# Last pair of down-projection rows: the two token halves of row 6 in separate PSUM tiles, its products in another order, all final multiplications on VectorE

## The chip, the core and the metric

The kernel runs on one core of a Trainium2 chip. The metric is the device time of one execution in microseconds. Three runs of the kernel before took 865.1, 865.74 and 865.78 us; the median is 865.74 us. The execution that the profiler recorded took 865.26 us, of which the span of its instructions covers 863.5 us; the 1.76 us around it belong to no instruction of the kernel.

## What is computed

One decoder block: a recurrent mixer, a state-space mixer, an output projection, a gated MLP, and a final RMSNorm. The change lies at the very end, in the MLP's down projection and the final norm:

```python
def conv_glu_ffn(h, w_up, conv_w, conv_b, w_down):
    u = causal_dwconv(h @ w_up, conv_w, conv_b)
    gate, val = jnp.split(u, 2, axis=-1)
    return (jax.nn.silu(gate) * val) @ w_down
...
    h = h + conv_glu_ffn(rmsnorm(h, norm2_w[l]), ...)
    y = rmsnorm(h, final_norm_w)
    return y[:, N_META:, :]
```

There are 512 tokens, 1024 model features and 2816 MLP features, all in float32.

## The kernel before

Features lie on the 128 partitions, tokens along the free axis. The 1024 model features make eight row tiles `hs[0]` to `hs[7]` (named `xr` in the profile), the 2816 MLP features make 22 tiles of the contraction. Every float32 product is made of three matmuls on rounded operands: weight-high times activation-high, weight-high times activation-low, weight-low times activation-high (`partial`, L1148 to L1150).

**Weights** come in chunks, in the order of the list `chunks`; `dn_chunks(p)` (L169 to L180) gives those of a pair of rows. A chunk passes three stages in `ahead` (L265): SyncE (SP) issues a DMA into a `raw` tile (L276), ScalarE (ACT) rounds it to `whi` (L199), VectorE (DVE) subtracts to get `wlo` (L200). Each of the three kinds of tile has three buffers. So the DMA of chunk n waits until `wlo` of chunk n-3 is made, and `whi` of chunk n waits until TensorE (PE) is through with chunk n-3. The next chunks are asked for two ahead of their use.

**Down projection.** Rows 0 and 1 are made plainly. Rows 2 to 7 are made in three pairs, p = 1, 2, 3 (loop at L1184, rows 2p and 2p+1). For the contraction tiles 8 to 19 a scheme with seven products is used in place of eight: chunks `d0` to `d6`, on halves of the 512 tokens, on sums of weights that were made in DRAM earlier (`sumsdn`), and on sums of activations (`dts`). The tiles 0 to 7 and 20, 21 go the plain way: chunks `qa` and `qb` for row 2p+1 at full width, chunks `ra` (8 tiles) and `rb` (2 tiles) for row 2p. The sums are:

- `x`: row 2p, first token half (first bank of a two-bank PSUM tile `pup`)
- `z`: row 2p, second token half (second bank of the same tile)
- `y`: a bank (`psn`) that is first set to a copy of `x` after `d0` (L1194), and whose content after `d2` is copied into `z` (L1200); with `s7` (copied from the bank `pv`) and `z` it gives the correction of row 2p+1 (L1207 to L1209)

For the last pair (`j == end`, rows 6 and 7) the list has `ra` and `rb` twice: `x` is finished first with one copy, then `z` gets `d4` and the other copy.

**Final norm.** When a row is complete, `squares` takes its square (L1174), multiplies it by the norm's weight (L1175) and adds the square to `facc` (L1177). Row 6 comes last and goes by token halves (L1228 to L1251): DVE adds the PSUM sum (L1231), ACT squares (L1232), PE sums over the partitions with a matrix of ones (L1235 for `facc`, L1236 for row 6), ACT takes logarithm and exponential (L1237, L1238), which gives `rs`, and eight rows are multiplied by `rs` into output tiles `ot`: rows 1 and 4 by GpSimd (POOL, L1247), row 6 by DVE with one more factor (L1244), the others by DVE (L1249). Two rows at a time go to DRAM by a 256 KB DMA, issued from SP for rows 0, 1 and 4, 5 and from ACT for rows 2, 3 and 6, 7 (L1251).

**What sets the order.** A scheduler places each engine's instructions before the program runs; on the chip each engine takes its own in that order. In the kernel before, the two adds of row 6 (L1231) stand side by side on DVE, behind all weight splits.

Of the kernel before, what the change touches and what calls it, by code (L numbers as in the profile page):

```python
# [11 lines left out]
ALU = mybir.AluOpType  # L12
# [12 lines left out]
KF = FF // P  # L25
# [18 lines left out]
C_FN = C_FB + 44  # L44
# [10 lines left out]
DN = 1, 2, 3  # L55
D0, DK = 8, 6
# [8 lines left out]
def tile_block(ctx: ExitStack, tc: tile.TileContext, xT, w_in, w_dt, w_out, w_up, w_down,  # L65
               par, consts, consti, out, dbg=None):
    nc = tc.nc
    V, A, G, PE = nc.vector, nc.scalar, nc.gpsimd, nc.tensor
# [9 lines left out]
    def slot(name, n=NT, dtype=F32, parts=P, tag="m"):  # L78
        return gp.tile([parts, n], dtype, tag=tag, name=name, bufs=TAGS[tag])
# [4 lines left out]
    def evac():  # L84
        return first(150000)

    def bank(name):
        return px.tile([P, 512], F32, tag="px", name=name)

    def banks2(name):  # L90
        return pj.tile([P, 1024], F32, tag="pj", name=name)
# [17 lines left out]
    def col(c):  # L109
        return pt[:, c:c + 1]  # L110
# [58 lines left out]
    def dn_chunks(p):  # L169

        j, j2, c1, c2, c3 = 2 * p, 2 * p + 1, D0 * P, (D0 + DK) * P, (D0 + 2 * DK) * P

        def summed(n):
            return lambda: sumd["dn", p][:, n * DK * P:(n + 1) * DK * P]

        rest = [(("ra", p), w_down[j][:, 0:c1], D0), (("rb", p), w_down[j][:, c3:], KF - D0 - 2 * DK)]
        r = [(("qa", p), w_down[j2][:, 0:c1], D0), (("d0", p), w_down[j][:, c1:c2], DK),
             (("qb", p), w_down[j2][:, c3:], KF - D0 - 2 * DK), (("d1", p), w_down[j][:, c2:c3], DK), (("d2", p), summed(0), DK),
             (("d3", p), summed(2), DK), (("d5", p), summed(1), DK), (("d6", p), w_down[j2][:, c2:c3], DK)]
        return r + (rest if p == DN[-1] else []) + [(("d4", p), summed(3), DK)] + rest  # L180

    for p in DN:
        chunks += dn_chunks(p)
# [81 lines left out]
    def ahead(n):  # L265
        while wnext[0] < min(n, len(chunks)):
            key, src, kc = chunks[wnext[0]]
            if key[0] in ("w0", "w1", "w2"):
                with first():
                    wdone[key] = scheme_weights(key)  # L270
                wnext[0] += 1
                continue
            with first(), ExitStack() as st:
                raw, hi, lo = raw_tiles(key)
                d = slice(0, kc * P)
                nc.sync.dma_start(raw[:, d], src() if callable(src) else src)  # L276
                if key[0] == "dn" and key[1] < 2 and not key[2]:
                    st.enter_context(tc.issue_after(last_s4[0].ins))
                split_weights(raw, hi, lo, d, V)
            wdone[key] = (hi, lo)  # L280
            wnext[0] += 1
# [13 lines left out]
    def weights(*key):  # L295
        if key in (("up", 0), ("up", KF)):
            return wdone.pop(key)
        used[0] += 1
        ahead(used[0] + 2)
        return wdone.pop(key)  # L300
# [29 lines left out]
    with first(200000):  # L330
        for k in range(0, KD, 2):
            d = slice(k * P, (k + 2) * P)
            for j, w, kx in ((BT, starts[0], k), (CT, starts[1], k + 1)):
                t = slot(f"x{kx}", tag="y")
# [37 lines left out]
    with first():  # L372
        for n, (a0, a1) in enumerate(((0, HALF), (HALF, NT))):
            p = bank(f"psn{n}")
# [4 lines left out]
        for k in range(KD):  # L379
            t = slot(f"xn{k}")  # L380
# [44 lines left out]
    for n, (a0, a1) in enumerate(((0, HALF), (HALF, NT))):  # L425
        p = bank(f"psd{n}")[0:66, :]
# [469 lines left out]
    hs, u2h, u2l = [], [], []  # L896
# [34 lines left out]
    u1 = []  # L931
# [69 lines left out]
    def product_banks(whole):  # L1001

        if not turn[0]:
            pairs.extend(banks2(f"pup{i}") for i in range(2))
        i = turn[0] % 2
        turn[0] += 1
        was, filled[i] = filled[i], whole
        return pairs[i], was
# [110 lines left out]
    dts = []  # L1119
    places = iter(["b1"] * 6 + ["L"] * 4 + ["u"] * 14)  # L1120
    first_half, second_half = slice(0, 256), slice(256, 512)
# [21 lines left out]
    def partial(ps, w, xs, start=False, stop=False):  # L1143

        for k, (xh, xl) in enumerate(xs):
            wh, wl = (t[:, k * P:(k + 1) * P] for t in w)
            one, end = start and k == 0, stop and k == len(xs) - 1
            PE.matmul(ps, wh, xh, start=one, stop=False, skip_group_check=True)  # L1148
            PE.matmul(ps, wh, xl, start=False, stop=False, skip_group_check=True)  # L1149
            PE.matmul(ps, wl, xh, start=False, stop=end, skip_group_check=True)  # L1150

    def gated(k0, kc, d):
        return [(ah[k][:, d], al[k][:, d]) for k in range(k0, k0 + kc)]

    def by_bank(t):
        return t.rearrange("p (a t) -> p a t", a=2)
# [25 lines left out]
    whole, K2, KR = slice(0, 512), D0 + DK, D0 + 2 * DK  # L1182
    end = 2 * DN[-1]
    for p in DN:  # L1184
        j, j2 = 2 * p, 2 * p + 1
        q = bank(f"pq{p}")
        partial(q[:], weights("qa", p), gated(0, D0, whole), start=True)
        xz, was = product_banks(True)
        assert was
        x, z, y, v = xz[:, first_half], xz[:, 512:768], u1[0][:, first_half], bank(f"pv{p}")[:, first_half]  # L1190
        sv, s7 = slot(f"dsv{p}", 512, tag="ab"), slot(f"ds7{p}", 256, tag="rs")
        partial(x, weights("d0", p), gated(D0, DK, first_half), start=True)
        with evac():
            A.activation(y, x, AF.Copy)  # L1194
        partial(q[:], weights("qb", p), gated(KR, KF - KR, whole), stop=True)
        V.tensor_tensor(hs[j2][:, META:], hs[j2][:, META:], q[:], ALU.add)
        partial(x, weights("d1", p), gated(K2, DK, first_half))
        partial(y, weights("d2", p), [t[1] for t in dts])
        with evac():
            A.activation(z, y, AF.Copy)  # L1200
        partial(v, weights("d3", p), [t[2] for t in dts], start=True, stop=True)
        with evac():
            A.activation(s7[:], v, AF.Copy)
        partial(z, weights("d5", p), [t[0] for t in dts])
        partial(y, weights("d6", p), [t[3] for t in dts], stop=True)
        with evac():
            V.tensor_tensor(sv[:, second_half], s7[:], z, ALU.add)  # L1207
            V.tensor_tensor(sv[:, first_half], s7[:], y, ALU.add)
        V.tensor_tensor(hs[j2][:, META:], hs[j2][:, META:], sv[:], ALU.subtract)  # L1209
        squares(j2)  # L1210

        def others(*sums):
            for key, k0, kc in (("ra", 0, D0), ("rb", KR, KF - KR)):
                w = weights(key, p)
                for ps, d in sums:
                    partial(ps, w, gated(k0, kc, d), stop=key == "rb")

        if j == end:
            others((x, first_half))
        partial(z, weights("d4", p), gated(K2, DK, second_half))  # L1220
        others(*([] if j == end else [(x, first_half)]), (z, second_half))
        if j < end:
            V.tensor_tensor(by_bank(hs[j][:, META:]), by_bank(hs[j][:, META:]), by_bank(xz[:])[:, :, first_half], ALU.add)
            squares(j)
            continue
        hh, halves, ps = hs[j], (0, 256), {0: x, 256: z}
        sq = slot(f"fsq{j}", 512, tag="pr")
        for d0 in halves:  # L1228
            d, dh = slice(d0, d0 + 256), slice(META + d0, META + d0 + 256)
            with evac():  # L1230
                V.tensor_tensor(hh[:, dh], hh[:, dh], ps[d0], ALU.add)  # L1231
                A.activation(sq[:, d], hh[:, dh], AF.Square)  # L1232
                p = bank(f"psn3_{d0}")
                rs = slot(f"rs{d0}", 256, tag="u")
                PE.matmul(p[:, 0:256], ones, acc[:, d], start=True, stop=False)  # L1235
                PE.matmul(p[:, 0:256], ones, sq[:, d], start=False, stop=True)  # L1236
                A.activation(rs[:], p[:, 0:256], AF.Ln, bias=eps[:], scale=1.0 / DM)  # L1237
                A.activation(rs[:], rs[:], AF.Exp, scale=-0.5)  # L1238
                pr = rs
                for k in range(0, KD, 2):  # L1240
                    ot = slot(f"ot{d0}_{k}", 512, tag="u")[:].rearrange("p (a t) -> p a t", a=2)
                    for i in range(2):
                        if k + i == end:
                            V.scalar_tensor_tensor(ot[:, i, :], hh[:, dh], col(C_FN + j), pr[:, 0:256],  # L1244
                                                   ALU.mult, ALU.mult)
                        elif k + i in (1, 4):
                            G.tensor_tensor(ot[:, i, :], hs[k + i][:, dh], rs[:], ALU.mult)  # L1247
                        else:
                            V.tensor_tensor(ot[:, i, :], hs[k + i][:, dh], pr[:, 0:256], ALU.mult)  # L1249
                    dst = out[k * P:(k + 2) * P, d].rearrange("(a p) t -> p a t", p=P)  # L1250
                    (nc.scalar if k % 4 else nc.sync).dma_start(dst, ot)  # L1251

# [64 lines left out]
```

## Time and profile before

| what | value |
|---|---|
| median of three runs | 865.74 us |
| the profiled execution's own time | 865.26 us |
| its span | 863.5 us |
| PE busy | 842.5 us (98% of the span) |
| DVE busy | 612.3 us (71%) |
| ACT busy | 485.7 us (56%) |
| POOL busy | 121.5 us (14%) |
| HBM read and written | 241 GB/s over the span |

A row of the timeline gives the start in microseconds from the span's start, the duration, the engine, the line, the operation, the tile written, the tiles read, and the sizes (partitions x elements). In brackets stands how long the engine had been idle, and what ended that. "SPq" and "ACTq" rows are the issue of a DMA, not its transfer. A row of the windows view gives a stretch, its length, the busy time of each engine with the number of instructions, the granted clock of PE as a share of full speed, and the busy share and rate of the DMA engines.

### The profile page before, as it was taken

What the parts mean: (1) busy time and instruction counts of PE and PEld (TensorE: products, weight loads), DVE (VectorE), ACT (ScalarE), POOL (GpSimd) and SP (SyncE); (2) the same over time, 40 slices, a digit from 0 to 9 for tenths busy, and PEclk for the clock granted to TensorE, in tenths of its full rate; (3) what the DMA queues carried; (4) which work ended last, traced back from release to release, by engine and by line L of the source; (5) the groups of instructions that cost most, each with busy time, mean ns of one, the idle gap of its engine ahead of it and who ended that gap; (6) DMA issues with size and microseconds to landing.
All of it is one profiled execution on the core that took longest, in us unless ns stands there. A gap on an engine that the chain in (4) does not pass through costs nothing. (4 is left out here: it accounts for less than half of the span.)

```text
span 863.5 us, 16958 instructions
## 1 busy us (share of the span) xinstructions
PE 842.5 (98%) x6908; PEld 812.9 (94%) x6908; DVE 612.3 (71%) x1036; ACT 485.7 (56%) x777; POOL 121.5 (14%) x160
## 2 busy tenths in 40 slices
PE   7999999999999999999999999999999999999994
PEld 6999899999999999999999999999999999889993
DVE  6984988799766666645353569878888888984554
ACT  8636985867444444454332345567666667653441
POOL 1321021222313131302222210000000000100001
PEclk9999999999999999999999999999999999999997
DMA  7598288783979598947987962365555555844552
GB/s 252 204 246 233 82 263 197 160 154 118 259 145 178 173 267 158 177 153 265 317 183 173 236 140 74 99 193 183 190 180 174 190 177 171 217 119 132 153 153 98
DMA packets 60143, 156.15 MB, mean 181 GB/s; under 512 B 6280, under 2 KB 10760, under 8 KB 60064
## 3 DMA queue, kind: packets, MB, share of 16 engines
q1 hardware_dynamic: 36704, 98.37, 34.7%
q0 software_dynamic: 20832, 53.09, 30.9%
q10 hardware_dynamic: 2528, 3.60, 1.3%
q8 instruction: 54, 0.88, 0.4%
q14 instruction: 25, 0.20, 0.1%
HBM read 152.89 MB, written 55.23 MB: 241 GB/s over the span
## 5 line engine op out<-in xcount | busy, mean ns | idle before, releaser
L322 PE MATMUL pj<-u_hi,whi_in 128*128 128x272 f32 (+1 forms) x752 | 156.6, 288 | 0.0
L322 PE MATMUL pj<-u_lo,whi_in 128*128 128x272 f32 (+1 forms) x752 | 156.5, 287 | 0.0
L322 PE MATMUL pj<-u_hi,wlo_in 128*128 128x272 f32 (+1 forms) x752 | 155.5, 286 | 0.0
L322 PEld LDWEIGHTS pj<-u_hi,whi_in 128*128 128x128 f32 x752 | 115.9, 188 | 2.8 <-issue 2.7
L322 PEld LDWEIGHTS pj<-u_lo,whi_in 128*128 128x128 f32 x752 | 116.0, 188 | 2.4 <-issue 1.8
L322 PEld LDWEIGHTS pj<-u_hi,wlo_in 128*128 128x128 f32 x752 | 116.3, 189 | 1.4 <-issue 1.3
L200 DVE TENSOR_TENSOR wlo_in<-raw_in,whi_in 128x1024 fp32r<-128x1024 f32 (+1 forms) x58 | 64.5, 1112 | 51.5 <-ACT whi_in L199 49.1
L199 ACT ACTIVATE whi_in<-raw_in 128x1024 fp32r<-128x1024 f32 (+1 forms) x58 | 56.1, 967 | 64.0 <-PE pj L322 59.1
L199 ACT ACTIVATE whi_w<-raw_w 128x1024 fp32r<-128x1024 f32 x54 | 57.2, 1058 | 26.4 <-PE pup L1052 13.3
L200 DVE TENSOR_TENSOR wlo_w<-raw_w,whi_w 128x1024 fp32r<-128x1024 f32 x54 | 66.0, 1222 | 6.4 <-ACT whi_w L199 5.8
L217 POOL COPY tick<-ticks 128x1 f32<-128x1 f32 x6 | 9.2, 1539 | 322.2 <-DVE ticks L216 322.2
L200 DVE TENSOR_TENSOR wlo_d<-raw_d,whi_d 128x768 fp32r<-128x768 f32 x21 | 20.1, 958 | 29.7 <-ACT whi_d L199 29.7
L1052 PE MATMUL psn<-t1l,whi_w 128*128 128x258 f32 x144 | 40.9, 284 | 0.0
L1053 PE MATMUL pup<-n_hi,wlo_w 128*128 128x258 f32 x144 | 40.8, 283 | 0.1
L1051 PE MATMUL pup<-n_hi,whi_w 128*128 128x258 f32 x144 | 40.8, 283 | 0.0
L1053 PE MATMUL psn<-t1h,wlo_w 128*128 128x258 f32 x144 | 40.7, 282 | 0.0
L1052 PE MATMUL pup<-n_lo,whi_w 128*128 128x258 f32 x144 | 40.6, 282 | 0.0
L1051 PE MATMUL psn<-t1h,whi_w 128*128 128x258 f32 x144 | 40.4, 280 | 0.0
L200 DVE TENSOR_TENSOR wlo_out<-raw_out,whi_out 128x1024 fp32r<-128x1024 f32 x16 | 19.6, 1225 | 26.4 <-ACT whi_out L199 26.4
L237 POOL DMA_DIRECT2D sums<-in_w_up_dram x18 | 21.2, 1179 | 114.6 <-issue 107.3
L199 ACT ACTIVATE whi_d<-raw_d 128x768 fp32r<-128x768 f32 x21 | 17.8, 848 | 32.9 <-PE pup L1149 15.6
L199 ACT ACTIVATE whi_out<-raw_out 128x1024 fp32r<-128x1024 f32 x16 | 16.9, 1055 | 25.9 <-PE pout L322 16.5
(459 smaller groups left out, 2570.5 us busy)
## 6 DMA issues: line engine op xcount, KB each, us to landing
sums<-in_w_up_dram POOLq DMA_DIRECT2D x54, 512.0 KB, 8.6
raw_in<-in_w_in_dram SPq DMA_DIRECT2D x50, 512.0 KB, 5.0
sums<-in_w_up_dram POOLq DMA_DIRECT2D x36, 256.0 KB, 7.9
raw_w<-in_w_up_dram SPq DMA_DIRECT2D x18, 512.0 KB, 3.5
raw_w<-sums SPq DMA_DIRECT2D x18, 512.0 KB, 4.0
raw_out<-in_w_out_dram SPq DMA_DIRECT2D x16, 512.0 KB, 6.5
sumsdn<-in_w_down_dram POOLq DMA_DIRECT2D x9, 768.0 KB, 8.1
sums<-sums POOLq DMA_DIRECT2D x18, 256.0 KB, 6.3
```

The lines of the kernel that those rows point to most:

```text
L199: A.activation(hi[:, d], raw[:, d], AF.Copy)
L200: eng.tensor_tensor(lo[:, d], raw[:, d], hi[:, d].bitcast(F32), ALU.subtract)
L217: gate = G.tensor_copy(tick[:], ticks[:, n:n + 1])
L237: G.dma_start(ds[j][:, 0:2], of[j][3], accum_op=ALU.add)
L322: PE.matmul(ps[:, O + a0:O + a1], w, x[:, a0:a1], start=s, stop=e)
L1051: PE.matmul(ps, wh, xh, start=first, stop=False, skip_group_check=True)
L1052: PE.matmul(ps, wh, xl, start=False, stop=False, skip_group_check=True)
L1053: last_product[:] = [PE.matmul(ps, wl, xh, start=False, stop=k == H - 1, skip_group_check=True)]
```

## The change

For the last pair alone: `z` moves into the other of the two `pup` tiles, so that `x` (`pup0`) and `z` (`pup1`) no longer share one. The weights that finish `x` get names and places of their own: `xb` (two tiles of the contraction) right behind `d1`, `xa` (eight tiles) behind `d5`. The products `d5` and `d6` swap places. So `x` is complete with `xa`, before `d4`. The count of matmuls, of weight chunks and of bytes stays the same. GpSimd's four multiplications go to DVE.

```diff
-        return r + (rest if p == DN[-1] else []) + [(("d4", p), summed(3), DK)] + rest
+        if p == DN[-1]:
+            r[6:8] = r[7], r[6]
+            xa, xb = [(key, *rest[n][1:]) for n, key in enumerate((("xa", p), ("xb", p)))]
+            r[4:4], r[9:9] = [xb], [xa]
+        return r + [(("d4", p), summed(3), DK)] + rest
...
-        x, z, y, v = xz[:, first_half], xz[:, 512:768], u1[0][:, first_half], bank(f"pv{p}")[:, first_half]
+        other = product_banks(True)[0] if j == end else xz
+        x, z, y, v = xz[:, first_half], other[:, 512:768], u1[0][:, first_half], bank(f"pv{p}")[:, first_half]
...
         partial(x, weights("d1", p), gated(K2, DK, first_half))
+        if j == end:
+            partial(x, weights("xb", p), gated(KR, KF - KR, first_half))
...
-        partial(z, weights("d5", p), [t[0] for t in dts])
-        partial(y, weights("d6", p), [t[3] for t in dts], stop=True)
+        for key in ("d6", "d5") if j == end else ("d5", "d6"):
+            if key == "d5":
+                partial(z, weights(key, p), [t[0] for t in dts])
+            else:
+                partial(y, weights(key, p), [t[3] for t in dts], stop=True)
...
         if j == end:
-            others((x, first_half))
+            partial(x, weights("xa", p), gated(0, D0, first_half), stop=True)
...
-                pr = rs
...
                         if k + i == end:
-                            V.scalar_tensor_tensor(ot[:, i, :], hh[:, dh], col(C_FN + j), pr[:, 0:256],
-                                                   ALU.mult, ALU.mult)
-                        elif k + i in (1, 4):
-                            G.tensor_tensor(ot[:, i, :], hs[k + i][:, dh], rs[:], ALU.mult)
+                            V.scalar_tensor_tensor(ot[:, i, :], hh[:, dh], col(C_FN + j), rs[:], ALU.mult, ALU.mult)
                         else:
-                            V.tensor_tensor(ot[:, i, :], hs[k + i][:, dh], pr[:, 0:256], ALU.mult)
+                            V.tensor_tensor(ot[:, i, :], hs[k + i][:, dh], rs[:], ALU.mult)
```

What this does to the order, at three places. First DVE, the end of its program before the change (`xr6` is row 6, `pup0` its PSUM tile, `ot0` and `ot256` the outputs of the first and the second token half, `rs0` and `rs256` their norms):

```order
L200 TENSOR_TENSOR wlo_ra_3_10145<-raw_ra_3_10143,whi_ra_3_10144 128x1024
L200 TENSOR_TENSOR wlo_rb_3_10157<-raw_rb_3_10155,whi_rb_3_10156 128x256
L1231 TENSOR_TENSOR xr6_5914<-xr6_5914,pup0_6048 128x256 x2
L1249 TENSOR_TENSOR ot0_0_10218<-xr0_5235,rs0_10213 128x256
L1249 TENSOR_TENSOR ot0_2_10222<-xr2_5418,rs0_10213 128x256
L1249 TENSOR_TENSOR ot0_2_10222<-xr3_5537,rs0_10213 128x256
L1249 TENSOR_TENSOR ot0_4_10226<-xr5_5785,rs0_10213 128x256
L1244 SCALAR_TENSOR_TENSOR ot0_6_10230<-xr6_5914,pt_75,rs0_10213 128x256
L1249 TENSOR_TENSOR ot0_6_10230<-xr7_6033,rs0_10213 128x256
L1249 TENSOR_TENSOR ot256_0_10242<-xr0_5235,rs256_10237 128x256
```

The same place with the change (its line numbers are a few higher: L1241 is the add that was L1231, L1255 and L1253 are the multiplications, L1181 is the sum into `facc`):

```order
L204 TENSOR_TENSOR wlo_ra_3_10127<-raw_ra_3_10125,whi_ra_3_10126 128x1024
L1181 TENSOR_TENSOR facc_9128<-facc_9128,fsq7_10121 128x512
L1241 TENSOR_TENSOR xr6_5914<-xr6_5914,pup0_6048 128x256
L204 TENSOR_TENSOR wlo_rb_3_10157<-raw_rb_3_10155,whi_rb_3_10156 128x256
L1255 TENSOR_TENSOR ot0_0_10218<-xr0_5235,rs0_10213 128x256
L1255 TENSOR_TENSOR ot0_0_10218<-xr1_5299,rs0_10213 128x256
L1255 TENSOR_TENSOR ot0_2_10222<-xr2_5418,rs0_10213 128x256
...
L1253 SCALAR_TENSOR_TENSOR ot0_6_10230<-xr6_5914,pt_75,rs0_10213 128x256
L1255 TENSOR_TENSOR ot0_6_10230<-xr7_6033,rs0_10213 128x256
L1241 TENSOR_TENSOR xr6_5914<-xr6_5914,pup1_6049 128x256
L1255 TENSOR_TENSOR ot256_0_10242<-xr0_5235,rs256_10237 128x256
```

The first half's add now stands ahead of the last weight split, all eight multiplications of the first half follow (those for rows 3 to 5 are left out here), and the second half's add stands behind them; `facc` is made behind the split of `ra`.

Second PE, with the change, from the end of `d4` on (`psn3_0` and `psn3_256` are the banks of the two sums over partitions, `cf` holds the ones):

```order
L1154 MATMUL pup1_6049<-ac19_hi_9032,wlo_d4_3_10096 128x256
L1152 MATMUL pup1_6049<-ac0_hi_7155,whi_ra_3_10126 128x256
L1153 MATMUL pup1_6049<-ac0_lo_7156,whi_ra_3_10126 128x256
L1154 MATMUL pup1_6049<-ac0_hi_7155,wlo_ra_3_10127 128x256
L1152 MATMUL pup1_6049<-ac1_hi_7287,whi_ra_3_10126 128x256
L1153 MATMUL pup1_6049<-ac1_lo_7288,whi_ra_3_10126 128x256
L1245 MATMUL psn3_0_10212<-facc_9128,cf_76 128x256
L1245 MATMUL psn3_256_10236<-facc_9128,cf_76 128x256
L1154 MATMUL pup1_6049<-ac1_hi_7287,wlo_ra_3_10127 128x256
L1152 MATMUL pup1_6049<-ac2_hi_7291,whi_ra_3_10126 128x256
```

Before the change the two sums over `facc` stood three matmuls ahead of the end of `d4`; now they stand five matmuls behind it. Three matmuls further on, behind `wlo_ra` of tile 2, comes the first half's sum over row 6 (L1246), which stood at the very end.

Third ACT, with the change, its last rows (L1242 is the square, L1247 and L1248 make `rs`):

```order
L203 ACTIVATE whi_ra_3_10126<-raw_ra_3_10125 128x1024
L1178 ACTIVATE fsq7_10121<-xr7_6033 128x512
L1179 ACTIVATE xr7_6033<-xr7_6033,pt_75 128x512
L203 ACTIVATE whi_rb_3_10156<-raw_rb_3_10155 128x256
L1242 ACTIVATE fsq6_10209<-xr6_5914 128x256
L1247 ACTIVATE rs0_10213<-psn3_0_10212,eps_78 128x256
L1248 ACTIVATE rs0_10213<-rs0_10213 128x256
L1257 DMA out_0_dram<-ot0_2_10222 128x2x256
L1257 DMA out_0_dram<-ot0_6_10230 128x2x256
L1242 ACTIVATE fsq6_10209<-xr6_5914 128x256
L1247 ACTIVATE rs256_10237<-psn3_256_10236,eps_78 128x256
L1248 ACTIVATE rs256_10237<-rs256_10237 128x256
```

The square of row 7 (L1178), which stood ahead of the split of the second `ra`, now stands behind it, and two output DMAs of the first half are issued ahead of the second half's square.

## The prediction

> **What bounds the kernel now.** I read the head of the page first: the span, and the share of PE.
>
> ```profile
> span 863.5 us, 16958 instructions
> PE 842.5 (98%) x6908; PEld 812.9 (94%) x6908; DVE 612.3 (71%) x1036; ACT 485.7 (56%) x777; POOL 121.5 (14%) x160
> ```
>
> PE is busy for 98% of the span, and the change adds or removes no matmul. So nothing is to be had while PE runs, unless PE is made to wait. What is left is the time behind the last matmul of the products. I therefore read the end of the chain of waits next (start, length, engine, tile, line).
>
> ```profile
> 845.04 0.86 PE psn L1235 x4
> 849.83 0.43 DVE xr L1231
> 850.28 0.42 ACT fsq L1232
> 850.75 0.71 PE psn L1236 x2
> 851.49 0.48 ACT rs L1237
> 852.00 0.43 ACT rs L1238
> 852.45 1.29 DVE ot L1249 x2
> 853.74 0.86 DVEq L1312
> 854.60 0.86 DVE ot L1249
> 855.46 0.86 DVE ot L1244
> 856.33 1.68 DVE ot L1249 x5
> 858.00 0.40 DVE ot L1244
> 858.40 0.34 DVE ot L1249
> ```
>
> From the add of row 6 at 849.83 to the first multiplication at 852.45 it is 2.62 us, through five instructions of which each waits for the one before. The multiplications end at 858.74, 6.29 us later. To the end of the span (863.5) it is another 4.76 us, in which no engine computes. In all 13.67 us, of which the change can hide the first half's share under matmuls.
>
> Two more views say what these 6.29 and 4.76 us are made of: the timeline of POOL, SP and ACT, and the windows (the last two columns are the share and rate of the DMA engines).
>
> ```profile
> 852.50 3.55 POOL L1247 TENSOR_TENSOR ot<-xr,rs 128x256 f32<-128x256 f32 x4 [101.87 <-ACT rs L1238]
> 853.48 0.40 SPq L1251 DMA_DIRECT2D out_dram<-ot  x1
> 858.76 0.38 ACTq L1251 DMA_DIRECT2D out_dram<-ot  x1
> 854.25:854.50 0.25, 0.00 (x0) 0.00 (x0) 0.25 (x1) 0.00 (x0) 0.25 (x2) 1.00 0.31 106
> 854.50:854.75 0.25, 0.00 (x0) 0.00 (x0) 0.25 (x2) 0.00 (x0) 0.25 (x1) 0.63 1.01 348
> 858.00:859.00 1.00, 0.00 (x0) 0.00 (x0) 0.73 (x3) 0.00 (x0) 0.00 (x0) 0.50 1.02 344
> 859.00:860.00 1.00, 0.00 (x0) 0.00 (x0) 0.00 (x0) 0.00 (x0) 0.00 (x0) 0.50 1.01 338
> 860.00:861.00 1.00, 0.00 (x0) 0.00 (x0) 0.00 (x0) 0.00 (x0) 0.00 (x0) 0.50 1.09 384
> 861.00:862.00 1.00, 0.00 (x0) 0.00 (x0) 0.00 (x0) 0.00 (x0) 0.00 (x0) 0.50 0.37 127
> ```
>
> While POOL works (to 856.05), DVE takes 0.86 us for a multiplication; later 1.68 / 5 = 0.336 us, and 0.40 for the one with a factor. And the DMA engines are full from 858 to 861.37 (the last window is 0.37 busy): the outputs pile up, and the last one, issued at 858.76, is written out 2.61 us later, at 861.37. From there to 863.5 it is 2.13 us.
>
> **The change part by part.** *The matmuls up to `x`.* I place them by the first matmul of `d1`, of `d4` and of the second `ra`, and the last of the products.
>
> ```profile
> 828.97 0.28 PE L1148 MATMUL pup<-ac_hi,whi_d 128*128 128x256 f32 x1
> 843.10 0.28 PE L1148 MATMUL pup<-ac_hi,whi_d 128*128 128x256 f32 x1
> 846.09 0.28 PE L1148 MATMUL pup<-ac_hi,whi_ra 128*128 128x256 f32 x1
> 849.51 0.28 PE L1150 MATMUL pup<-ac_hi,wlo_rb 128*128 128x256 f32 x1
> 850.75 1.13 PE L1236 MATMUL psn<-fsq,cf 128*128 128x256 f32 x4 [0.96 <-ACT fsq L1232]
> ```
>
> From 828.97 to 843.10 there are 120 matmuls without a gap: 14.13 / 120 = 0.1177 us each. With the change the same 120 stand there in another order: `d1` to 831.09, `xb` to 831.79, `d2` to 833.91, `d3` to 836.03, `d6` to 838.15, `d5` to 840.27, `xa` to 843.10. So `x` is complete at 843.10 either way; before, its add waited until 849.83. The reorder itself costs PE nothing as long as the weights arrive.
>
> *Do they arrive?* Here the rows of the three stages of a chunk, and what the page has for landings.
>
> ```profile
> 831.16 0.85 ACT L199 ACTIVATE whi_d<-raw_d 128x768 fp32r<-128x768 f32 x1 [1.38 <-PE pup L1149]
> 832.04 0.96 DVE L200 TENSOR_TENSOR wlo_d<-raw_d,whi_d 128x768 fp32r<-128x768 f32 x1 [1.07 <-ACT whi_d L199]
> 833.02 0.33 SPq L276 DMA_DIRECT2D raw_rb<-in_w_down_dram  x1
> 835.41 1.06 ACT L199 ACTIVATE whi_ra<-raw_ra 128x1024 fp32r<-128x1024 f32 x1 [1.00 <-PE pv L1149]
> 836.51 1.22 DVE L200 TENSOR_TENSOR wlo_ra<-raw_ra,whi_ra 128x1024 fp32r<-128x1024 f32 x1 [1.38 <-ACT whi_ra L199]
> 837.76 0.33 SPq L276 DMA_DIRECT2D raw_ra<-in_w_down_dram  x1
> 841.71 0.69 DVE L1177 TENSOR_TENSOR facc<-facc,fsq 128x512 f32<-128x512 f32 x1
> DMA to landing us min/median/max: 3.6/4.1/4.6
> raw_in<-in_w_in_dram SPq DMA_DIRECT2D x50, 512.0 KB, 5.0
> raw_out<-in_w_out_dram SPq DMA_DIRECT2D x16, 512.0 KB, 6.5
> ```
>
> The split at 831.16 starts as `d1` ends (831.09), and does so with the change, where the chunk is `d3`; its buffer comes free at 833.0, and SP issues the next DMA at 833.02. With the change that one is `xa`, 512 KB. The landing row is that of `raw_ra`, the same bytes from the same place: 3.6 us at least, 4.6 at most. I take 3.6, since at these points one load at a time is under way. So `xa` lands at 836.62 (its buffers are free at 836.03). By the `raw_ra` rows the split lasts 835.41 to 837.73, 2.32 us, so to 838.94, and 0.03 us later SP issues the last `ra`: 838.97. It lands at 842.57 and is split by 844.89. `facc` stands behind this split on DVE (0.69 us, and it starts about when the split ends): ready at about 845.55. PE comes to it five matmuls behind `d4`: 843.10 + 23 x 0.1177 = 845.81. So no wait, with 0.26 us to spare. That is where the change is tight, since `ra` is now loaded from 838.97 and used at 845.22 (843.10 + 18 x 0.1177); before, it was loaded from 837.76 and used at 846.09. What is queued behind a late `ra`: its split on ACT and DVE, the square of row 7, `facc`, the first half's add, and on PE everything to the end.
>
> *The first half.* The two sums over `facc` take 0.86 us (the first chain row): to 846.67. Four matmuls more: 847.14, and the first half's L1236 starts. Its square is made by then: the add follows `facc` on DVE at about 845.5 and is done at 845.95, the square 0.45 us later. From L1236 to the first multiplication the chain takes 852.45 - 850.75 = 1.70 us: 848.84. Eight multiplications, with POOL at rest: 7 x 0.336 + 0.40 = 2.75 us, to 851.59. PE ends its products meanwhile: 848.75 (843.10 + 48 x 0.1177) + 0.86 + 0.43 (half of the two sums) = 850.04, and some 0.2 us for the last result. **So it is DVE and no longer PE that holds the second half's add**: it stands behind the eight and starts at 851.59, not at 850.2.
>
> *The second half.* Add to first multiplication 2.62 us as before: 854.21. Eight more: 856.96. Before, the last ended at 858.74. In terms: a chain of 2.62 + 2.75 = 5.37 us in place of 8.91 (849.83 to 858.74) saves 3.54; the add starts 1.76 later; net **-1.78 us**.
>
> *POOL's four multiplications.* They are in this sum. Beside POOL, DVE took 852.45 to 856.33 for five multiplications, 3.88 us; alone they take 4 x 0.336 + 0.40 = 1.74. POOL so cost DVE 2.14 us, and spared it 4 x 0.336 = 1.34: without it 0.80 us are won over both halves. The Trainium skill, "Perfetto Trace Analysis", section "Optimizing Scalar/DVE Operations", says that a saturated DVE may hand work to GPSIMD, but that between these two it might not help as they share a port. By its first part the removal would cost DVE those 1.34 us and the gain would shrink by as much; the row of 0.86 against 0.336 speaks for the second part.
>
> *The outputs.* The first half's four DMAs are issued from 849.5 to 851.6 and are through when the second half's begin. The second half's pairs are ready at about 854.9, 855.6, 856.3 and 856.96. A DMA starts moving 0.9 us after its issue (853.48 to about 854.4) and 256 KB at 338 to 384 GB/s take 0.7 to 0.75 us; four in a row from 855.8 end at 858.8, or 1.85 us after the last multiplication, where it was 2.61 before (858.76 to 861.37, behind a queue of five). **-0.75 us**; from 0 (the same queue) to -0.9 (none at all).
>
> *Costs not in the trace.* ACT issues two of the first half's DMAs ahead of the second square. The last of them can go at 851.6 and its issue lasts 0.38 to 0.41 us, while the add ends at 852.02; I take nothing, at most 0.4 us. PE now rests from 850.2 to 852.5 before its last sum. In the windows the clock falls at about 854.57, which is 2.7 us after the last matmul's end (850.75 + 1.13); a rest of 2.3 us is short of it, so nothing; at half the clock the sum's 0.71 us would double, +0.7 at most. For that the Trainium skill, "TensorE: Matmul & The Clock Gate", section "HAM oscillation — how this bites in real kernels", gives a gap of more than about 3.4 us; by it there is still more room, and the 2.7 us of this trace is the stricter. The copy into `z`'s new tile waits for an add of pair 2, which stands on DVE ahead of the splits of `d1`: nothing.
>
> **The sum** is -1.78 - 0.75 = -2.5 us. On the profiled execution's own 865.26 us (863.5 and 1.76 around it) that is 862.8; on the median of 865.74 it is 863.2. I predict 863.0, between the two.
>
> **The rivals.** (a) *Late weights*: `xa` or `ra` lands later than 3.6 us. Everything behind shifts by what the two landings sum to over 7.2 + 0.26. For it: the same load took up to 4.6 us. With one such landing the time is 863.7, with two 864.7. (b) *Slower than before*: the same chain with landings as on the rest of the page, 5.0 us (`raw_in`) gives 10.0 - 7.46 = +2.5, hence no change (865.5); 6.5 us (`raw_out`) gives +5.5 and 868.5. The point from which it is slower is a sum of the two of 10.0 us. Against it: those are medians over the whole program, with POOL's own transfers beside them, while POOL at this end had been idle for 101.87 us (its row above). (c) *The halves do not overlap*, the change does not do what it says, and only POOL's 0.80 us and some 0.4 us of the outputs are won: 864.3. Against it: in DVE's order the first add stands ahead of the split of `rb`, which PE needs to finish `z`. (d) *More*: the eight multiplications do not hold the second add, and it starts at 850.2: 861.6. For that the first sum would have to stand 1.4 us earlier on PE; the order says it does not.
>
> **How the numbers follow.** A measurement of this kernel can tell about 0.2% from no change, so 864.0 is the bound to faster and 867.5 the bound to slower. The forecast as worked out, 862.3 to 864.0 with its unknown costs: 0.68. (a), mostly beyond 864.0: 0.14. (b): 0.08, of which 0.06 is beyond 867.5. (c): 0.06. (d): 0.04, below 862.3. The range 862.3 to 865.2 holds the forecast, (c) and all of (a). Faster 0.70 (the forecast, (d), less what the 0.4 us of ACT and 0.7 us of the clock can take from it), same 0.24, slower 0.06.
>
> **What would show it.** In the profile with the change: the first half's add at about 845.5, its first multiplication at 848.8, the eight in 2.75 us with no stretch of 0.86; the second add at 851.6, with DVE and not PE busy just before it; the last multiplication at 857.0, the last output issued right behind it, the DMA engines quiet between the halves. Wrong are my landings if PE is idle between 843 and 848, wrong is the wait on DVE if the second add follows PE's last product at once, and wrong is the term for the outputs if the span still ends 4.7 us behind the last multiplication.

## The result, and the profile after

The changed kernel took 863.64 us (median of 20 runs, 862.58 to 867.35), the kernel before on the same chip 865.76 us (20 runs). The ratio is 0.9975, with a 95% interval of 0.9964 to 0.9985: between 1.3 and 3.1 us faster, at the middle 2.2 us or 0.25%. Timed again later, beside the last experiments, the ratio was 0.9950 (0.9934 to 0.9966). The profiled execution has a span of 861.3 us, 2.2 us less than before.

Here is the end of the chain of waits with the change (start, length, engine, tile, line):

```profile
848.00 0.45 PE psn L1246 x2
848.47 0.48 ACT rs L1247
848.98 0.43 ACT rs L1248
849.43 2.10 DVE ot L1255 x6
851.53 0.40 DVE ot L1253
851.93 0.34 DVE ot L1255
852.26 0.34 DVE xr L1241
852.74 0.42 ACT fsq L1242
853.21 0.71 PE psn L1246 x2
853.95 0.48 ACT rs L1247
854.45 0.42 ACT rs L1248
854.90 0.42 DVE ot L1255
855.33 0.34 DVEq L1318
855.66 1.34 DVE ot L1255 x4
857.00 0.40 DVE ot L1253
857.39 0.34 DVE ot L1255
```

The first half's sum, norm and eight multiplications stand ahead of the second add (L1241), and the chain runs through them: the add of the second half is released by VectorE's own queue. PE had ended its products at 850.91, as its timeline shows in the last of these rows; the first is the start of `d4`, the other two are the sums over `facc` and the first half's sum.

```profile
843.81 0.28 PE L1152 MATMUL pup<-ac_hi,whi_d 128*128 128x256 f32 x1
846.51 1.02 PE L1245 MATMUL psn<-facc,cf 128*128 128x256 f32 x4
847.84 0.59 PE L1246 MATMUL psn<-fsq,cf 128*128 128x256 f32 x2
850.63 0.28 PE L1154 MATMUL pup<-ac_hi,wlo_rb 128*128 128x256 f32 x1
```

PE has no idle time between 843.81 and 850.91 (no row there has a bracket). The outputs, in the windows view (length, busy time of PE, PEld, DVE, ACT and POOL, granted clock, share and rate of the DMA engines):

```profile
857.00:858.00 1.00, 0.00 (x0) 0.00 (x0) 0.73 (x2) 0.00 (x0) 0.00 (x0) 0.50 1.04 348
858.00:859.00 1.00, 0.00 (x0) 0.00 (x0) 0.00 (x0) 0.00 (x0) 0.00 (x0) 0.50 1.09 380
859.00:859.50 0.50, 0.00 (x0) 0.00 (x0) 0.00 (x0) 0.00 (x0) 0.00 (x0) 0.50 0.96 334
859.50:860.00 0.50, 0.00 (x0) 0.00 (x0) 0.00 (x0) 0.00 (x0) 0.00 (x0) 0.50 0.04 10
```

The last multiplication ends at 857.73, the last packet at about 859.6, the span 1.7 us later.

**The measure for what follows.** Two executions differ by more than the change, long before the place of the change. The groups of the output projection's matmuls (L322, first and last start behind the count) show it, of before and of the experiment `tile_only`, whose programs are the same up to there:

```profile
L322 PE MATMUL pout<-ob_hi,whi_out x128: 277/281/288, 409.8 to 494.7; 128*128 128x258 f32 x64, 128*128 128x256 f32 x64
```

```profile
L322 PE MATMUL pout<-ob_hi,whi_out x128: 277/282/289, 413.6 to 498.4; 128*128 128x258 f32 x64, 128*128 128x256 f32 x64
```

It is 3.8 us at the start of this group; from there to the start of `d4` both take 433.3 us (843.10 and 846.90), and so do the other eight profiles. So neither the new tile nor the new order of the products costs PE anything before `d4`. So I compare the **closing stretch**, from the first matmul of `d4` to the end of the span, of each profile, and give the ratios of the times beside it. "Multiplied" is the end of the last multiplication, "written" the end of the last packet of the outputs. There is one profile of each kernel, and two of the change, which agree to 0.01 us.

| kernel | start of d4 | multiplied after | written after that | end after that | closing stretch | ratio of times |
|---|---|---|---|---|---|---|
| before | 843.10 | 15.64 | 2.72 | 2.03 | 20.38 | 1 |
| the change | 843.81 | 13.92 | 1.88 | 1.66 | 17.46 | 0.9975 (0.9964 to 0.9985) |
| after_again | 843.13 | 13.92 | 1.88 | 1.68 | 17.47 | 0.9950 (0.9934 to 0.9966) |
| split_only | 843.90 | 14.72 | 2.19 | 2.03 | 18.94 | 0.9973 (0.9962 to 0.9984) |
| pool_only | 845.38 | 14.92 | 2.29 | 1.65 | 18.85 | 0.9988 (0.9974 to 1.0001) |
| tile_only | 846.90 | 13.11 | 1.93 | 1.66 | 16.70 | 0.9966 (0.9952 to 0.998) |
| add_early | 846.11 | 12.57 | 1.88 | 1.67 | 16.13 | 0.9949 (0.9931 to 0.9967) |
| tail_best | 846.20 | 12.58 | 1.49 | 1.37 | 15.44 | 0.9943 (0.9924 to 0.9963) |
| pool_touch | 842.82 | 14.45 | 1.88 | 1.67 | 18.00 | one run |
| ra_late | 845.96 | 17.06 | 1.87 | 2.14 | 21.05 | one run |

### The profile page after: what moved, and what is told of

Same layout as the page of the kernel before. It is cut to its first block, busy times and chain, and to the rows that moved or that the text cites. A ratio compares the mean times of both kernels' runs of the same rounds, so it can differ in the third digit from the quotient of the medians.

```text
span 861.3 us, 16951 instructions
## 1 busy us (share of the span) xinstructions
PE 842.8 (98%) x6908; PEld 813.4 (94%) x6908; DVE 612.0 (71%) x1040; ACT 485.9 (56%) x777; POOL 117.8 (14%) x156
```

## The experiments

**split_only**: the change, with POOL's multiplications as before.

```diff
+                        elif k + i in (1, 4):
+                            G.tensor_tensor(ot[:, i, :], hs[k + i][:, dh], rs[:], ALU.mult)
```

> The change without its last part: GpSimd keeps its multiplications of rows 1 and 4, so two of each half's eight. The measure is the closing stretch, from the first matmul of d4 to the end of the span: 20.4 us before, 17.5 us with the whole change. Theory (GpSimd blocks VectorE while it reads): in each half VectorE's first two multiplications take 0.86 us beside GpSimd and the other four 0.336 and 0.40, 3.1 us in place of 2.75 to 2.8; the second half's add waits behind the first half's six, so the delay counts twice: closing stretch 18.2 to 18.3, about 0.7 us slower than the whole change. Rival (handing work to GpSimd relieves a VectorE that holds the end): six multiplications at 0.336 and 0.40, 2.1 us in each half, so 1.3 us faster than the whole change: 16.2.

Measured: closing stretch 18.94 us. The timeline of VectorE and of POOL in the first half:

```profile
849.51 2.51 DVE L1257 TENSOR_TENSOR ot<-xr,rs 128x256 f32<-128x256 f32 x4 [4.36 <-ACT rs L1248]
849.57 1.84 POOL L1255 TENSOR_TENSOR ot<-xr,rs 128x256 f32<-128x256 f32 x2 [98.51 <-ACT rs L1248]
```

VectorE's first four multiplications take 2.51 us; with the change six take 2.10. In all the multiplications end 0.80 us later than with the change, where the theory had about 0.7. The whole loss is 1.48 us; the other 0.68 us lie behind the multiplications (0.31 until the last packet, 0.37 from there to the end), and the theory did not have them. POOL's help costs more than it brings. The ratio of the times doesn't tell this kernel from the change; the closing stretch does.

**pool_only**: the kernel before, without POOL's multiplications.

```diff
-                        elif k + i in (1, 4):
-                            G.tensor_tensor(ot[:, i, :], hs[k + i][:, dh], rs[:], ALU.mult)
```

> The kernel before with one edit: VectorE makes all sixteen multiplications, nothing is split or reordered. Theory: the multiplications take 14 x 0.336 + 2 x 0.40 = 5.5 us in place of 6.29, and the outputs, which start earlier and without gaps, are written out by about 860.0 in place of 861.4 on the time axis of before: the closing stretch is 19.0 to 19.4 (20.4 before), the time 1.0 to 1.4 us below before. If the whole gain of the change came from this part it would be 17.5. Rival (GpSimd's help was worth its four multiplications): 1.3 us slower, 21.7.

Measured: 18.85 us. Compared with before, the multiplications end 0.72 us earlier (the prediction had 0.80 for this part), the outputs are written out 0.43 us sooner behind them, and the end follows 0.38 us sooner. So of the change's 2.92 us in the closing stretch, 1.53 come with POOL's part alone; the split of the halves brings the other 1.39, and 1.44 where POOL still works (20.38 to 18.94). The ratio of the times, whose interval reaches 1.0001, does not tell this kernel from before; the closing stretch does.

**add_early**: the change, with the second half's add (`adds[1]`) placed on VectorE behind four multiplications of the first half.

```diff
...
+        rs0 = norm(0)
+        outputs(0, rs0, (0, 2))
+        rs1 = norm(256)
+        with tc.issue_after(adds[1].ins):
+            outputs(0, rs0, (4, 6))
+        outputs(256, rs1, (0, 2, 4, 6))
```

> The change with another order on VectorE: the second half's add stands behind four of the first half's eight multiplications instead of behind all eight. Theory (VectorE's queue holds the second add, as worked out in the prediction; with the change it starts at 852.2 while the last matmul of the products ends at 850.9): the add starts at 850.9, the end comes 1.2 to 1.3 us earlier, closing stretch 16.2 to 16.4. Rival (the add waits for TensorE or for something else): 17.5, no change.

Measured: 16.13 us, 1.33 less than the change. VectorE's timeline and the last product on PE, and below them the row of the same add with the change:

```profile
852.92 0.28 PE L1154 MATMUL pup<-ac_hi,wlo_rb 128*128 128x256 f32 x1
853.24 0.42 DVE L1256 TENSOR_TENSOR xr<-xr,pup 128x256 f32<-128x256 f32 x1
853.58 0.75 DVE L1249 TENSOR_TENSOR ot<-xr,rs 128x256 f32<-128x256 f32 x2
```

```profile
852.18 0.41 DVE L1241 TENSOR_TENSOR xr<-xr,pup 128x256 f32<-128x256 f32 x1
```

The add follows the last product (853.20) at once. With the change it waited until 852.18, 1.27 us behind the product at 850.91. This 1.27 is the wait that the change put in the place of the one it removed.

**ra_late**: the change, with the load of the last `ra` made to wait for row 7 (`held[0]`).

```diff
...
+                if key == ("ra", DN[-1]):
+                    G.tensor_copy(raw[:, 0:1], held[0][:, META:META + 1])
...
```

> The change with the load of the last ra made late: GpSimd first copies one column of row 7 into the raw tile, which it can do at about 843.8, so the load is issued at 844 to 845 in place of 836.9. The scheduler then puts the two sums over facc and the first half's sum right behind d4. Theory (late weights hold TensorE, and with it the end): the load lands at 847.6 to 848.9, is split 2.3 us later, TensorE stands idle 2 to 4 us behind the sums, the products end at 853.1 to 854.4, the second add follows them at once and the closing stretch is 18.6 to 19.9. If the slack of this load is larger than that, TensorE does not wait, the first half's sum is 1.1 us earlier and the closing stretch 16.6.

Measured: 21.05 us, more than the theory's 18.6 to 19.9. PE waits where it said (rows of its timeline), for 2.4 us, where 2 to 4 were expected:

```profile
851.17 0.38 PE L1156 MATMUL pup<-ac_hi,whi_ra 128*128 128x256 f32 x1 [1.63 <-ACT whi_ra L203]
852.42 0.39 PE L1158 MATMUL pup<-ac_hi,wlo_ra 128*128 128x256 f32 x1 [0.76 <-DVE wlo_ra L204]
```

Most of the rest is the clock, third from the right in the windows view:

```profile
849.60:852.90 3.30, 0.98 (x6) 0.77 (x7) 1.75 (x3) 2.14 (x4) 0.00 (x0) 1.00 0.01 2
852.90:853.00 0.10, 0.10 (x3) 0.10 (x2) 0.10 (x2) 0.00 (x0) 0.00 (x0) 0.78 0.00 0
853.00:856.30 3.30, 3.30 (x18) 3.30 (x17) 2.45 (x8) 0.00 (x0) 0.00 (x0) 0.50 0.62 213
856.30:856.40 0.10, 0.10 (x2) 0.10 (x2) 0.00 (x0) 0.00 (x0) 0.00 (x0) 0.66 1.04 358
```

Behind the two waits it fell to half and stayed there for 3.4 us, though PE was busy all the time. A matmul took 0.213 us there in place of 0.118 (16 of them: 1.5 us). PE's last product ends 11.57 us after the start of `d4`, where it was 7.10 with the change: 4.47 us later, of which the waits are 2.4 and the clock 1.5. The last multiplication comes 3.14 us later, since with the change the second add waited another 1.27 us for VectorE anyway. So late weights do hold the end. This load was issued 0.38 us behind the start of `d4`, with the change 6.90 us ahead of it; delays shorter than these 7.3 us were not tried.

**tile_only**: the kernel before with the other PSUM tile for `z`, and without POOL's multiplications. The weights and products stay in the order of before.

```diff
...
+        other = product_banks(True)[0] if j == end else xz
-        x, z, y, v = xz[:, first_half], xz[:, 512:768], u1[0][:, first_half], bank(f"pv{p}")[:, first_half]
+        x, z, y, v = xz[:, first_half], other[:, 512:768], u1[0][:, first_half], bank(f"pv{p}")[:, first_half]
...
```

> The kernel before with two edits: z of the last pair in the other PSUM tile, and all multiplications on VectorE. The weights stay in the order of before (no xa and xb, d5 ahead of d6). Theory (x was complete at the first matmul of d4 before as well, and what held its add was the shared tile; the reorder of products brings nothing of its own): the halves overlap as with the whole change. The scheduler puts the first half's sum 20 matmuls and the two sums over facc behind the start of d4, where the change has it 27 and those sums behind it, so it starts 3.2 us behind the start of d4 in place of 4.0; VectorE ends the first half's eight 0.8 us earlier and the second add starts at 7.7 in place of 8.4; closing stretch (first matmul of d4 to the end of the span) 16.8 to 16.9, against 17.5 with the whole change. Rival (the reorder is what frees the first half): the first add waits for the second half, closing stretch 18.8 as measured with VectorE's multiplications alone.

Measured: 16.70 us, 0.76 less than the whole change, where the rival had the 18.85 of `pool_only`. The only difference from `pool_only` is the tile. The first row shows both adds of row 6 in `pool_only`, the second the first half's add here:

```profile
852.11 0.75 DVE L1231 TENSOR_TENSOR xr<-xr,pup 128x256 f32<-128x256 f32 x2 [4.70 <-PE pup L1150]
847.11 0.42 DVE L1232 TENSOR_TENSOR xr<-xr,pup 128x256 f32<-128x256 f32 x1 [0.92 <-PE pup L1150]
```

With the shared tile the add starts 6.73 us after the start of `d4` and waits for PE's last product; with a tile of its own it starts after 0.21 us. The shared tile alone had held the first half. The reorder brings nothing; with it the scheduler places the first half's sum 0.8 us later on PE, and since VectorE's queue holds the second add, that goes to the end. The times do not show this difference: the medians of this comparison are 864.37 us here and 862.46 for the change, but the intervals of the two ratios overlap, and `d4` started 3.8 us later in this profile.

**pool_touch**: the change with one more POOL instruction in the closing stretch.

```diff
+        G.tensor_copy(tick[:], acc[:, 0:1])
```

> The whole change, plus one GpSimd copy of a single column of facc into an unused column, right after facc is made, far from the path. In the runs so far the stretch from the last output's last packet to the end of the span is 2.1 us where GpSimd computed something in the closing stretch (before, split_only, ra_late) and 1.7 to 1.8 where it did not (after, pool_only, add_early). If that is GpSimd's doing: 2.1 here, closing stretch 17.8. If it came by chance or from the load of GpSimd's multiplications themselves: 1.7 to 1.8, closing stretch 17.5.

Measured: 1.67 us from the last packet to the end, so not every POOL instruction in the closing stretch brings the 2.1 us. The closing stretch was 18.00 nonetheless, by another cause, in one row of PE's timeline, the second half's sum:

```profile
852.22 1.22 PE L1247 MATMUL psn<-fsq,cf 128*128 128x256 f32 x2 [2.30 <-ACT fsq L1243]
```

It took 1.22 us in place of 0.70: the clock had fallen to half at 852.06, 2.1 us after the last product, in a rest that was as long (2.30 us) as with the change, where the clock held. Without these 0.52 us the closing stretch is 17.48.

**tail_best** and **after_again**: `add_early` with the second half's outputs written row by row, beside the change once more.

```diff
...
+                        if d0:
+                            r = k + i
+                            (nc.scalar if r % 2 else nc.sync).dma_start(out[r * P:(r + 1) * P, d], ot[:, i, :])
...
```

> add_early (second add behind four multiplications), and the second half's outputs written row by row, eight DMAs of 128 KB in turn from SP and ACT, in place of four of 256 KB. Theory (the outputs' transfers hold the end, and they can start when one row is ready): the first one is issued 0.34 us earlier, and the DMA engines, full until the end, end 0.3 to 0.35 us earlier: closing stretch 15.7 to 15.8 against 16.1 of add_early. If issuing eight DMAs costs more than it brings: 16.1 or more. In time about 3.5 to 4.5 us below before.

> The changed kernel once more, timed beside tail_best: closing stretch 17.5 us again (all instructions of that stretch have fixed durations), time about 2 us below before; the start of d4 may lie up to 2 us elsewhere, as it did among the runs so far, whose programs are the same up to there.

Measured: 15.44 us for `tail_best`: compared with `add_early`, the outputs are written 0.39 us sooner behind the last multiplication, as expected to within 0.1, and the end follows 0.3 us sooner, which was not. It has the shortest closing stretch of these kernels. Its median is 861.25 us, against 866.65 of before (ratio 0.9943, 0.9924 to 0.9963) and 862.46 of the change in the same comparison; the intervals of these two ratios overlap, so that it is faster than the change rests on the closing stretch. `after_again` has the closing stretch of the change to 0.01 us; its time is 4.2 us below before, where about 2 were expected.

## Why the prediction was right

The forecast was 863.0 us in a range of 862.3 to 865.2, and -2.5 us; the time is 863.64 us and -2.2 us, and the interval of 1.3 to 3.1 us faster holds the forecast. By its own steps:

- *PE loses nothing, `x` is complete at the start of `d4`.* Right: no idle time in PE's rows up to 850.91. `tile_only` adds what the step did not ask: the same holds without the reorder.
- *The weights, with 0.26 us to spare.* This step was wrong, without effect on the sum. It had SP issue the last `ra` behind the split of `xa`. But a raw tile waits for the chunk three before, and with the change that is `d5`. The rows of VectorE (the split of `d5`), SP and VectorE again (`facc`) show it:

```profile
835.93 0.96 DVE L204 TENSOR_TENSOR wlo_d<-raw_d,whi_d 128x768 fp32r<-128x768 f32 x1 [1.14 <-ACT whi_d L203]
836.91 0.33 SPq L280 DMA_DIRECT2D raw_ra<-in_w_down_dram  x1
843.39 0.68 DVE L1181 TENSOR_TENSOR facc<-facc,fsq 128x512 f32<-128x512 f32 x1
```

  The load of `xa` landed in the 3.6 us that the step took. The load of `ra` went out at 836.91; from the start of `d4` that is 2.8 us earlier than the step had it (838.97 with `d4` at 843.10). `facc` was ready at 844.07, and PE came to it at 846.51: 2.4 us to spare. So the 0.26 us that stood between the forecast and the rivals (a) and (b) were a tenth of the slack that there was, and their 0.22 was too much. Their mechanism is real: `ra_late` shows it, at a higher price than a plain shift, since the clock falls too.
- *The first half.* Right to 0.12 us. From the start of `d4`: its sum at 4.03 (4.04 forecast), the first multiplication at 5.62 (5.74), the second add at 8.37 (8.49). That VectorE and not PE holds this add is what the forecast rests on, and `add_early` shows it: 1.27 us, forecast 1.4.
- *The second half.* In the chain's rows, from the add at 852.26 to the first multiplication at 854.90, 2.64 us (2.62 forecast), then eight multiplications in 2.83 (2.75). Up to the last multiplication the change saves 15.64 - 13.92 = 1.72 us; the forecast was 1.78.
- *POOL.* Forecast 0.80 us; `pool_only` gave 0.72 in the order of before, `split_only` 0.80 with the halves apart. The runs bear out the warning half of what the prediction cites from the Trainium skill ("Perfetto Trace Analysis", "Optimizing Scalar/DVE Operations"), and not the advice to hand work over.
- *The outputs.* Forecast -0.75 us, measured 2.72 to 1.88, -0.84. The first half's four DMAs were through by 854.2, before the second half's began to move at 856.6, as the step said.
- *The clock.* The prediction put the rest of 2.3 us before the last sum at nothing, because in the profile before the clock fell 2.7 us after the last matmul. It came out so in both profiles of the change, but by luck of when the rest fell: in `pool_touch` a rest of the same length cost 0.52 us (see the hardware section).
- *Not forecast*: from the last packet to the end 0.37 us less.
- *The sum* is -1.72 - 0.84 - 0.37 = -2.9 us in the closing stretch, against -2.5. That the span fell by 2.2 us only is the start of `d4`, 0.7 us later in this profile, which comes from the first 100 us, where nothing was changed. The two timings, -2.2 and -4.2 us at their medians, lie on both sides of 2.9. So the mechanism was right, and that the first timing came within 0.3 us of the forecast was in part luck.
- *Rival (c)*, that the halves do not overlap, is out by the chain after. *Rival (d)*, a second add that waits for PE alone, did not come true, but it can be had: `add_early` is that case.

## What to carry to other kernels

When a long chain at the end is cut in two and one part is hidden, look at what the hidden part puts into an in-order queue ahead of the other: here eight multiplications stood before the one add that mattered, and moving that add forward brought another 1.3 us. Two sums that are read at different times belong in different tiles: in this kernel that, and not the order of the products, was what freed the first half. Where the order of loads changes, count the buffers to find which chunk a load waits for, and ask of each new rest of TensorE what the clock does after it.

## What the runs showed of the hardware

**The clock changes at fixed intervals of 3.41 us, and not after a rest of a fixed length.** In `ra_late` it fell at 852.96, rose at 856.37 and fell again at 863.20: 3.41 us, and 6.83, twice that. In the clock records of all ten traces the stretches between two changes last 3.41, 6.83, 75.09, 764.59, 768.00 or 843.09 us, which are 1, 2, 22, 224, 225 and 247 times 3.413 us. Before the first fall in `ra_late` PE rested for 1.63 and 0.76 us and was busy for 0.98 of the last 3.3 us. Once down, the clock stayed for a whole interval of full work. With the change, the interval that ended at 852.02 (3.41 us ahead of the fall at 855.43) held 2.3 us of work, and the clock held; in `pool_touch` the interval that ended at 852.06 took in more of an equally long rest, held 1.3 us of work, and the clock fell. So the last sum's 0.5 us are a matter of where the rest falls in the interval. The prediction's 2.7 us, read off one fall, was no threshold. How little work is too little stays open: at the end of the kernels the clock held after intervals with 1.9 to 2.8 us of work, but at about 85 us it fell in five profiles after intervals with 2.0 to 2.4.

The figure of about 3.4 us in the Trainium skill ("TensorE: Matmul & The Clock Gate", "HAM oscillation — how this bites in real kernels") fits the interval here, while its reading as the length of one idle gap does not: half the clock came after gaps of 1.6 and 0.8 us.

**From the last packet to the end of the span it is 1.4 to 2.1 us.** It is 2.03 in the two kernels in which POOL multiplies beside VectorE (before and `split_only`), 1.65 to 1.68 in six others and 1.37 in `tail_best`. But it is 2.14 in `ra_late` and 1.67 in `pool_touch`, where POOL copied one column 17 to 21 us before the end. What sets it stays open.

**The first 410 us vary by up to 4 us** between executions of the same instructions (409.55 to 413.55 at the output projection, in the ten profiles). Most of it arises at one place. At about 83 us PE comes to a matmul that waits for a tile named `btk` from ScalarE: not at all in before, `after_again` and `pool_touch`, 0.40 and 0.51 us in the change and `split_only`, 0.97 to 1.76 in the other five. In these five, and in no other, the clock then stands at half for 3.41 us. Here are the row of the wait with the change and in `tile_only`, and the window behind it in before and in `tile_only`:

```profile
83.18 1.12 PE L585 MATMUL psu<-xdc,btk 16*128 16x512 f32 x2 [0.40 <-ACT btk L559]
84.23 1.12 PE L581 MATMUL psu<-xdc,btk 16*128 16x512 f32 x2 [1.76 <-ACT btk L555]
85.00:90.00 5.00, 5.00 (x36) 4.28 (x34) 3.25 (x6) 5.00 (x14) 0.00 (x0) 1.00 0.43 166
85.00:90.00 5.00, 5.00 (x22) 3.90 (x22) 2.59 (x4) 5.00 (x18) 0.00 (x0) 0.67 0.63 244
```

All five profiles whose `d4` starts after 845 are these five. Why the wait differs between executions was not looked into.
